# The adaLN modulation of a hybrid decoder layer as one-row matmuls in four column strips

## The chip, the cores and the metric

The kernel runs on one core of one Trainium2 chip. Its engines work beside each other from programs of their own: TensorE (PE, matmuls into the accumulators called PSUM; PEld is its weight load), VectorE (DVE), ScalarE (ACT), GpSimd (POOL, idle here) and SyncE (SP), which issues all DMAs here. The metric is the device time of one execution in microseconds (us); lower is better.

## The reference, cut to what matters

One decoder layer for 256 tokens of width 2048, all in float32:

```python
c_act = silu(c)                                   # (1, 2048)
mod = c_act @ w_ada + b_ada                       # w_ada: 2048 x 12288, 96 MB
sh1, sc1, g1, sh2, sc2, g2 = split(mod, 6)
h = layer_norm(x) * (1 + sc1) + sh1
mix = token_mix(h, ...)                           # w_in 2048 x 4160, attention (A), latent attention (B), w_o
x = layer_norm(alpha * x + g1 * mix)
h = layer_norm(x) * (1 + sc2) + sh2
ffn = peer(h, w_pq, sub_keys, u_table, v_table)   # 16384 experts of width 2048, top 16 of 8 heads
x = layer_norm(alpha * x + g2 * ffn)
```

The modulation is one row of 2048 numbers times a matrix: 12288 dot products, of which each number of the 96 MB of weights is read once.

## The kernel before, in words

The 2048 channels lie as 16 blocks of 128 on the partitions. The weights come in pieces of 1 MB. In most products a piece is split on the fly: ACT casts it to a short form `hi` (line 98), DVE forms the rest `lo` (line 100), and TensorE runs three matmuls of the short type for each product, hi by hi, lo by hi and hi by lo (`mm3`, lines 136 to 139). Some pieces go unsplit as float32 matmuls: 12 of the 32 pieces of `w_in` (`F32_PIECES`, line 330) and three of the latents' pieces (`LAT_F32`: uk0 and uq1 in line 154, uqr in line 147).

The modulation is done on DVE. `ada(pool, tag, bufs, j)` (line 203) loads the 1 MB of weights that make 128 of the 12288 outputs, with the outputs on the partitions, and multiplies it by silu(c), which `spread_cols` has spread over all partitions (`cb`), in two halves with a running sum (line 208). `ada_bias` (line 211) adds the halves and the bias into `modc`, one column for each block of 128 outputs. 32 such loads (shift 1 and scale 1) are needed before the rows of `w_in` that they modulate; 48 (gate 1, shift 2, scale 2) are drawn one by one at fixed places through attention and the output projection by `ada_pull`, from two buffers; 16 (gate 2) come in the second half of the kernel.

`w_in` is worked off in four groups `kg` of 512 of its 2048 rows. `group_start` modulates four blocks of the normalised input (ACT, line 301), splits them (lines 157 and 158) and multiplies them by the 64 columns of `w_kr` (line 306, result with the tokens on the partitions in two PSUM banks). `w_in_pieces` then multiplies eight pieces; after each, `ada_in` takes up one load of the next group's modulation. Attention follows with projections between its heads, then `w_o`, the norm, `w_pq`, the expert tables `u` (lines 132, 133) and `v`.

A scheduler orders the instructions of each engine when the program is built, and each engine then runs its list strictly in that order. A tile's buffer is handed on when its last reader is done: for a modulation weight that is DVE before the change.

Of the kernel before, what the change touches and what calls it, by code (L numbers as in the profile page):

```python
# [10 lines left out]
F32 = mybir.dt.float32  # L11
# [50 lines left out]
def tile_hybrid_peer_block(ctx: ExitStack, tc: tile.TileContext, a, out):  # L62
# [5 lines left out]
    psum = ctx.enter_context(tc.tile_pool(name="psum", bufs=2, space=PSUM))  # L68

    def bank(tag, name):  # L70
        return psum.tile([P, 512], F32, tag=tag, name=name, bufs=4 if tag == "mm" else 2)

    def banks8(name):
        return [bank(("mm", "mm", "mm", "mm", "tr", "tr", "sm", "sm")[i], f"{name}{i}") for i in range(8)]

    def bcast_row(dst, src_row):
        n = dst.shape[-1]
# [125 lines left out]
    def ada(pool, tag, bufs, j):  # L203

        w = pool.tile([P, D], F32, tag=tag, name=f"ada{j}", bufs=bufs).rearrange("p (z n) -> p z n", z=2)
        nc.sync.dma_start(w, a["w_ada"][j].rearrange("p (z n) -> p z n", z=2))
        for z in range(2):
            nc.vector.scalar_tensor_tensor(w[:, z, :], w[:, z, :], 1.0, cb[:, z * 1024:(z + 1) * 1024], op0=ALU.mult,  # L208
                                           op1=ALU.mult, accum_out=(modc, modh)[z][:, j:j + 1])

    def ada_bias(j0, n):
# [26 lines left out]

    with tc.tile_pool(name="front", bufs=1) as front:
        def ada_rest():  # L240
            for j in range(G1, SH2):
                ada(front, "ada", 2, j)
                yield
            ada_bias(G1, 16)
            for kg in range(4):
                for i in range(4):
                    for j0 in (SH2, SC2):
                        ada(front, "ada", 2, j0 + 4 * kg + i)
                        yield
                for j0 in (SH2, SC2):  # L250
                    ada_bias(j0 + 4 * kg, 4)

        rest = ada_rest()

# [17 lines left out]
        with tc.tile_pool(name="mix", bufs=1) as mix, ExitStack() as attn_pool:  # L272
# [9 lines left out]
            nc.scalar.activation(cols[:, V_C:V_C + KC], cols[:, V_C:V_C + KC], AF.Silu)  # L282
            spread_cols(cb, cols[:, V_C:V_C + KC], "c")
            for th in range(2):
                mv, r = ln_stats(mix, xn[th])
# [8 lines left out]
            def modulate(kg, h, kw, half):  # L294
                hs = slice(2 * half, 2 * half + 2)
                ks = slice(4 * kg + 2 * half, 4 * kg + 2 * half + 2)
                for j0 in (SH1, SC1):
                    ada_bias(j0 + 4 * kg + 2 * half, 2)
# [10 lines left out]
            kr_ps = [bank("sm", f"kr_ps{th}") for th in range(2)]  # L309

            def w_in_pieces(kg, ns, act):

# [33 lines left out]
            def ada_in(kg, m):  # L346
# [5 lines left out]
                    return ada(mix, f"xt{m % 2}", 1, j)  # L352
                return ada((early_a, early_b)[m % 2], "raw", 1, j)

            def group_start(kg):
# [15 lines left out]
            for m in range(4, 8):  # L371
                ada_in(0, m)
            for kg in range(3):
                h = group_start(kg)
                m = 0
                for ns in IN_ORDER[kg]:
                    w_in_pieces(kg, ns, h)
                    while m < ns[-1] + 1:
                        ada_in(kg + 1, m)
                        m += 1  # L380
            early_pools.close()
            hmod3 = group_start(3)

# [131 lines left out]
            def latents():  # L515
                w_in_pieces(3, (6, 7), hmod3)
                ada_pull(PULLS[0])
                krd = mix.tile([P, 2, 2, 64], F32, tag="kw", name="krd")
                for th in range(2):
                    nc.scalar.copy(krd[:, th, 0, :], kr_ps[th][:, :64])  # L520
# [9 lines left out]
                krT = attn.tile([P, T], F32, name="krT")  # L530
# [228 lines left out]
    with tc.tile_pool(name="back", bufs=1) as back:  # L759
# [24 lines left out]
        with tc.tile_pool(name="sel", bufs=1) as sel:  # L784
# [108 lines left out]
            def scatter(th, on_vector):  # L893

                for tb in range(8 * th, 8 * th + 8):
                    stg = sel.tile([P, NKEY, 16], F32, tag="stg", name=f"stg{tb}", bufs=2)
                    for b in range(4):
                        ps = bank(("sm", "tr")[b % 2], f"g_ps{tb}_{b}")
# [196 lines left out]
def _layout(i):  # L1095
    def tiles(w, n):
# [11 lines left out]
        "consts": _consts(),  # L1108
        "cols": cont(cols.T),
        "x": cont(i["x"].reshape(2, P, D)),  # L1110
        "w_ada": cont(i["w_ada"][0].reshape(D, 96, P).transpose(1, 2, 0)),
        "w_in": tiles(w_in[:, :4096], 512),
        "w_kr": cont(w_in[:, 4096:].reshape(4, 4, P, 64).transpose(0, 2, 1, 3)),
# [28 lines left out]
```

## Time and profile before

| | |
|---|---|
| three timed runs | 2072.48, 2075.01, 2075.48 us; median 2075.01 us |
| the profiled execution | 2072.09 us, its span 2070.3 us |
| TensorE busy, clock granted | 2002.6 us (97%), 0.983 |
| DVE, ACT busy | 1434.0 us (69%), 1027.9 us (50%) |
| HBM read | 473.40 MB |

Busy time of TensorE overstates its work, because matmuls are pipelined and their ends are modelled; what a matmul costs in a stream is the distance from start to start. A float32 matmul call stands in the trace as two records (each with its own weight load): the 96 calls of line 330 are 192 records. The granted clock is given as a share of 2.4 GHz; at 0.5 it is 1.2 GHz. "Who waited for whom" lists idle time of an engine with what ended it.

### The profile page before, as it was taken

How to read it: one execution, taken by the hardware profiler on the slowest of the kernel's cores; microseconds unless marked ns; L12 is line 12 of the kernel's file. 1: busy time of each engine (PE TensorE's matmuls, PEld its weight loads, DVE VectorE, ACT ScalarE, POOL GpSimd, SP SyncE). 2: the span in 40 equal slices, each digit the busy share in tenths (PEclk: the TensorE clock that was granted, in tenths of full speed). 3: DMA queues.
4: the chain of work that ended last, by engine and by line, in shares of the span. 5: the costliest groups of instructions: out<-in, count | busy, mean ns of one | idle time of the engine just before them, and what ended most of it. 6: DMA issues, size and time to landing. Idle time of an engine off the chain costs nothing.

```text
span 2070.3 us, 26806 instructions
## 1 busy us (share of the span) xinstructions
PE 2002.6 (97%) x10328; PEld 1672.8 (81%) x10329; DVE 1434.0 (69%) x2509; ACT 1027.9 (50%) x1478; POOL 0.2 (0%) x4
## 2 busy tenths in 40 slices
PE   6999998979999999999999999999999999999997
PEld 3567686769988888899888888888888888888886
DVE  7589978889799677677765454477766555445457
ACT  2323457445554877866444444454444454444441
POOL 0000000000000000000000000000000000000000
PEclk8999999989999999999999999999999999999999
DMA  9787887858445555666885555578876656555552
GB/s 364 314 328 311 328 323 262 345 234 318 184 157 190 194 212 193 224 204 214 291 280 190 198 188 198 188 266 306 300 286 244 224 205 235 192 202 184 203 203 102
DMA packets 100864, 496.13 MB, mean 240 GB/s; under 512 B 7792, under 2 KB 41728, under 8 KB 42880
## 3 DMA queue, kind: packets, MB, share of 16 engines
q1 hardware_dynamic: 100736, 494.41, 64.8%
q8 instruction: 81, 1.33, 0.2%
q14 instruction: 47, 0.39, 0.1%
HBM read 473.40 MB, written 20.98 MB: 239 GB/s over the span
## 4 chain that ended last, share of the span: by engine, by line
PE 93%; DVE 5%; ACT 1%; issue 0%; DMA 0%; SPq 0%; DVEq 0%; ACTq 0%
PE u_ps L132 23%; PE u_ps L133 12%; PE v_ps L138 11%; PE v_ps L137 11%; PE v_ps L139 11%; PE win_ps L330 3%; PE g_ps L914 3%; PE win_ps L138 2%; PE win_ps L139 2%; PE wpq_ps L138 2%; PE wpq_ps L139 2%; DVE ada L208 2%; PE wpq_ps L137 1%; PE win_ps L137 1%; PE wo_ps L139 1%; PE wo_ps L138 1%
## 5 line engine op out<-in xcount | busy, mean ns | idle before, releaser
L132 PE MATMUL u_ps<-act,hi_u 128*128 128x512 f32 x2048 | 727.8, 400 | 3.0 <-DVE W L779 3.0
L133 PE MATMUL u_ps<-act,lo_u 128*128 128x256 f32 x2048 | 574.0, 280 | 0.0
L100 DVE TENSOR_TENSOR lo_v<-raw_v,hi_v 128x1024 fp32r<-128x1024 f32 x244 | 298.2, 1224 | 264.4 <-ACT hi_v L98 264.3
L132 PEld LDWEIGHTS u_ps<-act,hi_u 128*128 128x128 f32 x2048 | 386.1, 189 | 95.2 <-DVE W L779 3.3
L100 DVE TENSOR_TENSOR lo_u<-raw_u,hi_u 128x1024 fp32r<-128x1024 f32 x256 | 312.1, 1222 | 179.8 <-ACT hi_u L98 178.8
L98 ACT CAST hi_v<-raw_v 128x1024 fp32r<-128x1024 f32 x244 | 257.2, 1054 | 327.8 <-PE v_ps L139 321.3
L133 PEld LDWEIGHTS u_ps<-act,lo_u 128*128 128x128 f32 x2048 | 387.6, 189 | 0.0
L137 PE MATMUL v_ps<-hi_v,whi 128*128 128x512 f32 x976 | 379.7, 389 | 0.0
L138 PE MATMUL v_ps<-lo_v,whi 128*128 128x512 f32 x976 | 379.7, 389 | 0.0
L139 PE MATMUL v_ps<-hi_v,wlo 128*128 128x512 f32 x976 | 379.7, 389 | 0.0
L98 ACT CAST hi_u<-raw_u 128x1024 fp32r<-128x1024 f32 x256 | 267.6, 1048 | 212.5 <-PE u_ps L132 193.4
L208 DVE SCALAR_TENSOR_TENSOR ada<-ada,cb 128x1024 f32<-128x1024 f32 x192 | 229.0, 1219 | 12.2 <-DMA ada<-in_w_ada_dram 12.0
L137 PEld LDWEIGHTS v_ps<-hi_v,whi 128*128 128x128 f32 x976 | 183.2, 188 | 38.3
L139 PEld LDWEIGHTS v_ps<-hi_v,wlo 128*128 128x128 f32 x976 | 183.2, 188 | 38.0
L138 PEld LDWEIGHTS v_ps<-lo_v,whi 128*128 128x128 f32 x976 | 183.2, 188 | 37.8
L330 PE MATMUL win_ps<-raw_win,hmod 128*128 128x512 f32 x192 | 87.2, 610 | 1.2 <-ACT hmod L301 1.2
L912 DVE TENSOR_SCALAR o<-iota,i2T,gT 128x128 f32<-128x128 f32 x256 | 72.9, 342 | 19.9 <-PE g_ps L914 19.8
L137 PE MATMUL wpq_ps<-act,hi_wpq 128*128 128x256 f32 x256 | 72.7, 286 | 1.9 <-ACT act L157 1.9
L138 PE MATMUL wpq_ps<-act,hi_wpq 128*128 128x256 f32 x256 | 73.1, 286 | 0.4 <-DVE act L158 0.4
L778 ACT COPY W<-u_ps 128x256 f32<-128x256 f32 x128 | 47.3, 369 | 52.3 <-PE u_ps L133 51.8
L139 PE MATMUL wpq_ps<-act,lo_wpq 128*128 128x256 f32 x256 | 72.8, 285 | 0.0
L330 PEld LDWEIGHTS win_ps<-raw_win,hmod 128*128 128x128 f32 x192 | 36.9, 196 | 43.8 <-issue 42.0
(319 smaller groups left out, 2316.1 us busy)
## 6 DMA issues: line engine op xcount, KB each, us to landing
raw_u<-in_u_dram SPq DMA_DIRECT2D x128, 1024.0 KB, 4.8
raw_v<-in_v_dram SPq DMA_DIRECT2D x122, 1024.0 KB, 4.8
ada<-in_w_ada_dram SPq DMA_DIRECT2D x96, 1024.0 KB, 5.9
raw_win<-in_w_in_dram SPq DMA_DIRECT2D x32, 1024.0 KB, 8.4
raw_wo<-in_w_o_dram SPq DMA_DIRECT2D x16, 1024.0 KB, 6.9
raw_wpq<-in_w_pq_dram SPq DMA_DIRECT2D x16, 1024.0 KB, 6.0
g_d<-stg SPq DMA_DIRECT2D x16, 1024.0 KB, 4.9
gl<-g_d SPq DMA_DIRECT2D x16, 1024.0 KB, 6.8
```

What stands on the lines that cost most here:

```text
L98: nc.scalar.copy(hi, raw[:, 2 * j:2 * j + 2, :])
L100: nc.vector.tensor_sub(lo, raw[:, 2 * j:2 * j + 2, :], hi.bitcast(F32))
L132: nc.tensor.matmul(pss[e], hi[:, i, es], act[:, k], start=first and j == 0 and i == 0, stop=False)
L133: nc.tensor.matmul(pss[e][:, 1], lo[:, i, es], act_hi[:, k, :], start=False, stop=last and j == 1 and i == 3)
L137: nc.tensor.matmul(o, sh, mh, start=start, stop=False)
L138: nc.tensor.matmul(o, sh, ml, start=False, stop=False)
L139: nc.tensor.matmul(o, sl, mh, start=False, stop=stop)
L208: nc.vector.scalar_tensor_tensor(w[:, z, :], w[:, z, :], 1.0, cb[:, z * 1024:(z + 1) * 1024], op0=ALU.mult, op1=ALU.mult, accum_out=(modc, ...
L330: nc.tensor.matmul(ps[th], act[:, i, ts], src[:, i, :], start=i == 0, stop=i == 3)
L778: nc.scalar.copy(ws[:, e], pss[e][:, 1])
L912: nc.vector.tensor_scalar(o2, iota, i2T[:, t:t + 1], gT[:, t:t + 1], op0=ALU.is_equal, op1=ALU.mult)
L914: nc.tensor.matmul(ps[:, q * P:(q + 1) * P], o1[:, q, :], o2, start=True, stop=True)
```

## The change

All of the modulation but gate 2 (80 of the 96 loads) becomes matmuls with one output row. silu(c) of one block of 128 channels is the stationary operand, one column wide, and 512 columns of a row block of `w_ada` stream by. Four row blocks write to output partitions 0, 32, 64 and 96 of one PSUM bank (the four column strips), and four 1 MB tiles, of four row blocks each, accumulate there. ACT copies the bank to SBUF, four matmuls by a matrix of ones and zeros (`strips`) add the four rows up and turn the result from a row into columns, and one DVE instruction adds the bias. That is a group: 512 outputs, 4 tiles, 16 matmuls, 1 copy, 4 small matmuls, 1 DVE instruction. There are 18 groups; the first 1024 outputs come from eight tiles in another cut (`first_ada`, 64 matmuls of 256 columns).

Further: 2 instead of 12 pieces of `w_in` and none of the latents stay float32; the product with `w_kr` is turned round (64 output rows by 256 tokens, two column halves in one bank), with a repair for its layout in `latents`; the PSUM bank thus freed holds the modulation. The weights are laid out anew for this on the host, with the same bytes.

```diff
-F32_PIECES = (4, 3, 2, 3)
+F32_PIECES = (2, 0, 0, 0)
-LAT_F32 = ('uk0', 'uq1', 'uqr')
+LAT_F32 = ()
...
-        return psum.tile([P, 512], F32, tag=tag, name=name, bufs=4 if tag == "mm" else 2)
+        return psum.tile([P, 512], F32, tag=tag, name=name, bufs={"mm": 4, "tr": 2, "sm": 1, "ad": 1}[tag])
...
+    def ada_group(ps, ws, tiles, strips, j0):
+        for q in range(4):
+            p, tag, bufs = tiles[q]
+            w = p.tile([P, 4, 512], F32, tag=tag, name=f"ada{j0}_{q}", bufs=bufs)
+            nc.sync.dma_start(w, ws[q])
+            for g in range(4):
+                nc.tensor.matmul(ps[32 * g:32 * g + 1, :], c1[:, 4 * q + g:4 * q + g + 1], w[:, g, :], start=q == 0,
+                                 stop=q == 3)
+            if q < 3:
+                yield
+        rows = stream.tile([P, 2, 512], F32, tag="lo", name=f"ada_rows{j0}", bufs=4)[:, 0, :]
+        nc.scalar.copy(rows, ps)
+        yield
+        for i in range(4):
+            nc.tensor.matmul(ps[:, 2 * i:2 * i + 2], rows[:, i * P:(i + 1) * P], strips[:, 2:4], start=True, stop=True)
+        one = 1.0 if (SC1 <= j0 < G1 or SC2 <= j0 < G2) else 0.0
+        nc.vector.scalar_tensor_tensor(modc[:, j0:j0 + 4], ps[:, 0:8:2], one, cols[:, j0:j0 + 4], op0=ALU.add,
+                                       op1=ALU.add)
...
         def ada_rest():
-            for j in range(G1, SH2):
-                ada(front, "ada", 2, j)
-                yield
-            ada_bias(G1, 16)
...
+            order = [G1 + 4 * g for g in range(4)] + [j + 4 * g for g in range(4) for j in (SH2, SC2)]
+            for j0 in order:
+                yield from ada_group(ada_ps, a["w_ada_r"][j0 // 4], [(front, "ada", 2)] * 4, strips, j0)
...
                 for i in range(2 * half, 2 * half + 2):
-                    for th in range(2):
-                        nc.tensor.matmul(kr_ps[th][:, :64], h[:, i, th * P:(th + 1) * P], kw[:, i, :],
-                                         start=(kg == 0 and i == 0), stop=(kg == 3 and i == 3))
+                    g = 64 * (i % 2)
+                    nc.tensor.matmul(kr_ps[g:g + 64, :T], kw[:, i, :], h[:, i, :], start=(kg == 0 and i < 2),
+                                     stop=(kg == 3 and i >= 2))
...
+            def first_ada(half):
...
+                    for which in range(2):
+                        ada_rows(ps, ws[which], which, part)
...
-            for m in range(4):
-                ada_in(0, m)
+            first_ada(0)
...
             for kg in range(3):
                 h = group_start(kg)
                 m = 0
+                if ON_PE:
+                    slots = [(front, "ada", 2)] * 2 + [(mix, f"xt{m}", 1) for m in range(2)]
+                    work = [ada_group(ada_ps, a["w_ada_r"][j0 // 4 + kg + 1], slots, strips, j0 + 4 * kg + 4)
+                            for j0 in (SH1, SC1)]
+                    work = itertools.chain(*work)
                 for ns in IN_ORDER[kg]:
                     w_in_pieces(kg, ns, h)
                     while m < ns[-1] + 1:
-                        ada_in(kg + 1, m)
+                        if ON_PE:
+                            next(work, None)
```

Where the work moves on TensorE shows in its list, in which a number after an L is a line of its own kernel (lines 138 to 140 after are `mm3`, 137 to 139 before). First the passage from group 0 of `w_in` to group 1, before: `win_ps` are the products with `w_in`, `kr_ps` those with `w_kr`.

```order
L139 MATMUL win_ps_7_1_498<-hi_win_7_1_505,act 128x512
L306 MATMUL kr_ps_232<-kw_540,hmod_539 128x64 [waits DMAHW5_49]
L306 MATMUL kr_ps_233<-kw_540,hmod_539 128x64
L306 MATMUL kr_ps_232<-kw_540,hmod_539 128x64 [waits Activation_49]
L330 MATMUL win_ps_0_0_566<-raw_win_0_572,hmod_539 128x512 [waits DMAHW6_49]
```

After, in the same place; `ada_ps` is the bank of the modulation, `ada_rows` its copy in SBUF:

```order
L140 MATMUL win_ps_7_1_626<-hi_win_7_1_633,act 128x512
L233 MATMUL ada_ps<-ada_3_663,cols 1x512 [waits DMAHW4_49]
L233 MATMUL ada_ps<-ada_3_663,cols 1x512 x3
L241 MATMUL ada_ps<-strips,ada_rows_669 128x2 [waits Activation_49]
L241 MATMUL ada_ps<-strips,ada_rows_669 128x2 x3
L344 MATMUL kr_ps<-hmod_676,kw_677 64x256 [waits DMAHW5_49,Activation_49]
L138 MATMUL win_ps_0_0_691<-hi_win_0_0_699,act 128x512 [waits Activation_49]
L139 MATMUL win_ps_0_0_691<-lo_win_0_0_701,act 128x512 [waits DVE_49]
```

The last tile of the modulation that group 1 needs, and its strips, stand directly ahead of the group's own products. Second, the start of the latent attention heads, before: `s_b` are scores, `uv_ps` a projection ahead of them.

```order
L139 MATMUL uv_ps_1853<-hi_uv_1_1860,act 128x512
L561 MATMUL s_b_1894<-qk_1180 128x128 [waits Activation_49]
L562 MATMUL s_b_1894<-krT,qk_1180 128x128
L563 MATMUL s_b_1894<-qk_1180 128x256
L564 MATMUL s_b_1894<-krT,qk_1180 128x256
L561 MATMUL s_b_1934<-qk_1180 128x128 [waits Activation_49]
```

After, with the tiles of one group of the modulation between the heads:

```order
L140 MATMUL uv_ps_2322<-hi_uv_1_2329,act 128x512
L233 MATMUL ada_ps<-ada_1_2359,cols 1x512 [waits DMAHW3_49]
L639 MATMUL s_b_2365<-qk_1461 128x128 [waits Activation_49]
L640 MATMUL s_b_2365<-krT,qk_1461 128x128
L641 MATMUL s_b_2365<-qk_1461 128x256
L642 MATMUL s_b_2365<-krT,qk_1461 128x256
L233 MATMUL ada_ps<-ada_2_2391,cols 1x512 [waits DMAHW6_49]
L639 MATMUL s_b_2416<-qk_1461 128x128 [waits Activation_49]
```

Each tile's four matmuls stand alone between matmuls of full width, and wait for their own load. Over the whole list TensorE changes between calls of different shape of the array (128 rows by 128, 64 or 32 columns, or 64 rows) 34 times before and 198 times after.

## Rows read from the trace of the kernel before

**Rows 1.** The page's head: span, busy time by engine, clock in 40 slices.

```profile
span 2070.3 us, 26806 instructions
...
PE 2002.6 (97%) x10328; PEld 1672.8 (81%) x10329; DVE 1434.0 (69%) x2509; ACT 1027.9 (50%) x1478; POOL 0.2 (0%) x4
...
PEclk8999999989999999999999999999999999999999
```

**Rows 2.** The page's chain that ended last, share by engine.

```profile
PE 93%; DVE 5%; ACT 1%; issue 0%; DMA 0%; SPq 0%; DVEq 0%; ACTq 0%
```

**Rows 3.** Windows: stretch, length, busy us (count) by engine, clock, DMA share, GB/s.

```profile
45.00:250.00 205.00, 197.99 (x732) 132.55 (x731) 166.25 (x284) 71.72 (x104) 0.00 (x0) 0.98 0.80 322
250.00:325.00 75.00, 74.14 (x408) 58.04 (x407) 60.71 (x167) 41.49 (x99) 0.00 (x0) 1.00 0.81 314
325.00:475.00 150.00, 125.37 (x577) 99.79 (x577) 130.11 (x278) 83.53 (x138) 0.00 (x0) 0.91 0.72 282
475.00:600.00 125.00, 121.82 (x934) 118.55 (x935) 109.41 (x349) 59.74 (x73) 0.00 (x0) 0.96 0.60 227
600.00:2071.00 1471.00, 1458.05 (x7583) 1246.42 (x7581) 933.27 (x1351) 758.11 (x1044) 0.00 (x0) 1.00 0.61 218
```

**Rows 4.** Timeline of TensorE, float32 `w_in` pieces: start, length, count.

```profile
91.96 20.82 PE L330 MATMUL win_ps<-raw_win,hmod 128*128 128x512 f32 x48
```

**Rows 5.** Line 330 by itself: count, duration min/median/max in ns.

```profile
L330 PEld LDWEIGHTS win_ps<-raw_win,hmod x192: 186/190/337, 28.2 to 235.6; 128*128 128x128 f32 x192
L330 PE MATMUL win_ps<-raw_win,hmod x192: 591/592/1167, 28.2 to 236.0; 128*128 128x512 f32 x192
```

**Rows 6.** Windows, `win_ps` alone, split pieces only.

```profile
116.00:136.00 20.00, 20.00 (x90) 16.56 (x89) 4.80 (x7) 0.00 (x0) 1.00 0.97 388
```

**Rows 7.** Timeline of TensorE, a split projection of 256 columns.

```profile
263.13 0.28 PE L137 MATMUL uq_ps<-act,hi_uq 128*128 128x256 f32 x1
...
265.53 0.28 PE L139 MATMUL uq_ps<-act,lo_uq 128*128 128x256 f32 x1
```

**Rows 8.** Timeline of TensorE at the passage to group 1: the product with w_kr.

```profile
90.23 1.89 PE L306 MATMUL kr_ps<-kw,hmod 128*128 128x64 f32 x16
```

**Rows 9.** Timeline of TensorE, scores of latent heads; 64*128 is half the array's rows.

```profile
284.27 0.49 PE L562 MATMUL s_b<-krT,qk 64*128 64x128 f32 x2
284.69 0.70 PE L563 MATMUL s_b<-qk 128*128 128x256 f32 x2
285.32 0.70 PE L564 MATMUL s_b<-krT,qk 64*128 64x256 f32 x2
285.94 0.49 PE L561 MATMUL s_b<-qk 128*128 128x128 f32 x2
```

**Rows 10.** Instruction groups of DVE up to 700 us: the modulation.

```profile
L208 DVE SCALAR_TENSOR_TENSOR ada<-ada,cb 128x1024 f32<-128x1024 f32 x160 | 190.9, 1219 | 10.0 <-DMA ada<-in_w_ada_dram 9.8
```

**Rows 11.** Who waited for whom, TensorE, 45 to 600 us: total, times, longest.

```profile
PE h_ps L712 <- ACT xc L709: 10.7, 2, 6.9
PE win_ps L138 <- DVE lo_win L100: 5.6, 4, 2.9
PE pt_a L434 <- DVE mx_a L429: 4.9, 4, 3.6
```

**Rows 12.** Timeline, all engines, second half of group 0's modulation.

```profile
39.76 0.16 DVE L215 SCALAR_TENSOR_TENSOR modc<-modc,cols 128x2 f32<-128x2 f32 x1
39.95 1.09 ACT L301 ACTIVATE hmod<-xnT,modc 128x256 f32<-128x256 f32 x2 [10.70 <-DVE modc L215]
...
41.08 0.62 ACT L157 CAST act<-hmod 128x512 fp32r<-128x512 f32 x1
...
41.73 0.69 DVE L158 TENSOR_TENSOR act<-hmod,act 128x512 fp32r<-128x512 f32 x1 [1.81 <-ACT act L157]
...
50.46 0.59 ACT L340 COPY proj<-win_ps 128x512 f32<-128x512 f32 x1 [8.76 <-PE win_ps L330]
```

**Rows 13.** DMA issues of the page: count, KB each, median us to landing.

```profile
ada<-in_w_ada_dram SPq DMA_DIRECT2D x96, 1024.0 KB, 5.9
```

More of the change, by code (lines that the diff above doesn't have):

```diff
@@ L70, in bank @@
     def bank(tag, name):
-        return psum.tile([P, 512], F32, tag=tag, name=name, bufs=4 if tag == "mm" else 2)
+        return psum.tile([P, 512], F32, tag=tag, name=name, bufs={"mm": 4, "tr": 2, "sm": 1, "ad": 1}[tag])
     def banks8(name):
-        return [bank(("mm", "mm", "mm", "mm", "tr", "tr", "sm", "sm")[i], f"{name}{i}") for i in range(8)]
+        return [bank(("mm", "mm", "mm", "mm", "tr", "tr", "sm", "ad")[i], f"{name}{i}") for i in range(8)]
     def bcast_row(dst, src_row):
@@ L209, in ada, with silu_strips, ada_rows @@
                                            op1=ALU.mult, accum_out=(modc, modh)[z][:, j:j + 1])
+    c1 = cols[:, V_C:V_C + KC]
+    def silu_strips(pool):
+        ps = bank("ad", "ada_ps")
+        nc.vector.memset(ps, 0.0)
+        strips = pool.tile([P, 4], F32, name="strips")
+        nc.vector.memset(strips, 0.0)
+        for g in range(4):
+            nc.vector.memset(strips[32 * g:32 * g + 1, g // 2:g // 2 + 1], 1.0)
+            nc.vector.memset(strips[32 * g:32 * g + 1, 2:4], 1.0)
+        return ps, strips
+    def ada_group(ps, ws, tiles, strips, j0):
[3 more added lines that the diff above has]
+            nc.sync.dma_start(w, ws[q])
+            for g in range(4):
+                nc.tensor.matmul(ps[32 * g:32 * g + 1, :], c1[:, 4 * q + g:4 * q + g + 1], w[:, g, :], start=q == 0,
[10 more added lines that the diff above has]
+                                       op1=ALU.add)
+    def ada_rows(ps, w, which, half):
+        for i in range(8):
+            g = 32 * (2 * which + i % 2)
+            k = 8 * half + i
+            nc.tensor.matmul(ps[g:g + 1, :256], c1[:, k:k + 1], w[:, i, :], start=half == 0 and i < 2,
+                             stop=half == 1 and i >= 6)
     def ada_bias(j0, n):
@@ L297, in modulate @@
                 for j0 in (SH1, SC1):
-                    ada_bias(j0 + 4 * kg + 2 * half, 2)
+                    if kg > 0 and not ON_PE:
+                        ada_bias(j0 + 4 * kg + 2 * half, 2)
                 for i in range(2 * half, 2 * half + 2):
@@ L304, in modulate @@
                 for i in range(2 * half, 2 * half + 2):
[L305 to L309 removed]
+                    g = 64 * (i % 2)
+                    nc.tensor.matmul(kr_ps[g:g + 64, :T], kw[:, i, :], h[:, i, :], start=(kg == 0 and i < 2),
+                                     stop=(kg == 3 and i >= 2))
+            kr_ps = bank("sm", "kr_ps")
             def w_in_pieces(kg, ns, act):
@@ L353, in ada_in @@
                 return ada((early_a, early_b)[m % 2], "raw", 1, j)
+            def first_ada(half):
+                ps = ada_ps
+                for part in range(2):
+                    ws = []
+                    for which in range(2):
+                        m = 4 * half + 2 * part + which
+                        where = (0, 2, 1, 0)[m // 2]
+                        pool, tag, bufs = ((front, "ada", 2), (mix, f"xt{m % 2}", 1),
+                                           ((early_a, early_b)[m % 2], "raw", 1))[where]
+                        w = pool.tile([P, 8, 256], F32, tag=tag, name=f"ada0_{m}", bufs=bufs)
+                        nc.sync.dma_start(w, a["w_ada0"][half, which, part])
+                        ws.append(w)
+                    for which in range(2):
+                        ada_rows(ps, ws[which], which, part)
+                rows = stream.tile([P, 2, 512], F32, tag="lo", name=f"first_rows{half}", bufs=4)[:, 0, :]
+                nc.scalar.copy(rows[:, :256], ps[:, :256])
+                for i in range(2):
+                    nc.tensor.matmul(ps[:, 256 + 2 * i:258 + 2 * i], rows[:, i * P:(i + 1) * P], strips[:, 0:2], start=True,
+                                     stop=True)
+                for which, (j0, one) in enumerate(((SH1, 0.0), (SC1, 1.0))):
+                    j = j0 + 2 * half
+                    nc.vector.scalar_tensor_tensor(modc[:, j:j + 2], ps[:, 256 + which:260:2], one, cols[:, j:j + 2],
+                                                   op0=ALU.add, op1=ALU.add)
             def group_start(kg):
@@ L366, in tile_hybrid_peer_block @@
             early_b = early_pools.enter_context(tc.tile_pool(name="early_b", bufs=1))
-            for m in range(4):
-                ada_in(0, m)
+            first_ada(0)
             for n in range(2):
                 first[0, n] = load_piece(a["w_in"][0, n], f"win0_{n}")
-            for m in range(4, 8):
-                ada_in(0, m)
+            first_ada(1)
             for kg in range(3):
@@ L378, in tile_hybrid_peer_block @@
                     while m < ns[-1] + 1:
-                        ada_in(kg + 1, m)
+                        if ON_PE:
+                            next(work, None)
+                        else:
+                            ada_in(kg + 1, m)
                         m += 1
+                if ON_PE:
+                    for _ in work:
+                        pass
             early_pools.close()
@@ L518, in latents @@
                 krd = mix.tile([P, 2, 2, 64], F32, tag="kw", name="krd")
+                krs = attn.tile([P, T], F32, name="krT")
+                nc.scalar.copy(krs, kr_ps[:, :T])
+                both = attn.tile([P, 64], F32, name="both")
+                nc.vector.tensor_add(both, ident[:, 0:64], ident[:, 64:128])
                 for th in range(2):
-                    nc.scalar.copy(krd[:, th, 0, :], kr_ps[th][:, :64])
+                    nc.tensor.matmul(kr_ps[:, 256 + th * 64:320 + th * 64], krs[:, th * P:(th + 1) * P], both, start=True,
+                                     stop=True)
+                    nc.scalar.copy(krd[:, th, 0, :], kr_ps[:, 256 + th * 64:320 + th * 64])
                 nc.sync.dma_start(cst, a["consts"][:, C_COSA:])
```

16 lines of the change are left out of this document (7 added, 9 removed).

## The prediction, made before the kernel was run

> **What bounds the kernel now.** I read the page's head first, then its chain, then windows by stage, then rows of single lines. TensorE is busy 97% of the span and its clock is granted nearly throughout [rows 1]; the chain that ended last is TensorE for 93% [rows 2]. A busy share can hide idle time, so the test is the distance from start to start: 48 float32 records take 20.82 us, less the last one's own 0.59 that is 0.430 us each [rows 4, 5], and 90 records of the split pieces start in 20.00 us, 0.222 us each [rows 6]. Those streams are dense; no faster engine beside them would shorten them. The windows say where TensorE has idle time after its start: 7.0 us from 45 to 250, 0.9 to 325, 24.6 to 475, 3.2 to 600 [rows 3], 35.7 us in all. DVE works 190.9 us on the modulation [rows 10], but of TensorE's waits those that end with DVE come to 5.6 and 4.9 us; the longest total, 10.7, ends with ACT [rows 11]. DVE is full, and yet hardly in the way.
>
> So 190.9 us are taken from an engine with little on the path, and work is put on the engine that is the path. Everything hangs on how much TensorE time the column strips take.
>
> **The change part by part.** The sum is made on the profiled execution's 2072.09 us, 2.9 under the median of 2075.01.
>
> *Float32 pieces become split ones.* A piece was 8 calls, 16 records: 16 x 0.430 = 6.88 us. Split it is 24 x 0.222 = 5.33. Ten pieces of w_in and uqr save 1.55 each, 17.1 us. uk0 and uq1 have 256 columns: 32 records at half of 0.430 are 6.88; split they are 48 at 0.120 (20 steps in 2.40 us [rows 7]), 5.76; two save 2.2. Together -19.3. ACT and DVE get the casting of 13 pieces more; DVE has the room, since it loses 190.9.
>
> *The product with w_kr.* 64 records at 1.89/16 = 0.118 [rows 8] were 7.6 us. Now 16 calls of 256 columns, 32 records at 0.215, are 6.9 one after the other and 3.4 if the two halves run beside each other as I assume below for the strips. -4 (bounds -0.7 to -6).
>
> *The strips.* The first 1024 outputs wait for their loads before and after: 0. The other 18 groups have 72 tiles, each four calls of 512 columns. A float32 call is two records (192 for 96 calls [rows 5]), both on the same strip. No row of before shows a narrow call, so I bound a tile. One after the other its 8 records take 8 x 0.430 = 3.44 us. With four strips fully side by side only the two passes of one strip are left: 0.86. Between them lies what TensorE's order makes likely: records start in the order of the program, and the second pass of strip 0 stands ahead of the first of strip 32 and needs strip 0 free. Then each call adds one pass, not a quarter: first pass, then four steps, 5 x 0.430 = 2.15 us. I take that: 72 x 2.15 = +155 us; the ends are +62 and +248.
>
> The Trainium skill (TensorE: Matmul & The Clock Gate, section on packing small matmuls) says that matmuls start and end strictly in program order, and gives 2.38x for three column strips measured. The order would give my middle value; the speedup, taken as 3x for four strips, gives about 1.15 us a tile, 83 us, and an end some 72 us earlier. No row here shows strips, so neither is tested yet.
>
> *Change of shape.* Where full calls alternate with calls on half of the rows, two records of 256 columns take 0.63 and 0.62 us from start to start instead of 0.43 [rows 9]: 0.2 us for each change of shape. The list has 198 such changes instead of 34. 164 x 0.2 = +33 us (bounds 0, if columns differ from rows in this, and 33).
>
> *Adding up.* Four calls for each group with two columns by a full weight load, 144 records; the nearest row is w_kr's narrow call at 0.118 [rows 8]: +17 (bounds 8 and 31, at 0.215).
>
> *New waits.* The last tile of a group of w_in now stands directly ahead of that group's products. From the bias to the split input took 2.5 us (39.92 to 42.42 [rows 12]), and ACT's copy of the bank, 0.59 for that shape [rows 12], comes ahead of it; the products with w_kr fill about a half of a microsecond. Before, those products followed without a gap [rows 8]. I take 3 us at each of three passages: +9 (bounds 3 and 15). In the list a tile also waits for its load, which takes 5.9 us [rows 13], with two buffers that come free only when TensorE has read them. Queued behind it is all of TensorE. Between uv and the heads three tiles stand close together, and likewise near w_pq. The single bank makes the next group wait for DVE's bias. I take +10 (bounds 0 and 25; the end is 12 groups at about 2 us).
>
> *Given back.* Some tiles fall into the 35.7 idle microseconds [rows 3], and waits for DVE shrink. -25 (bounds 0 and -36). What is late next in those places is ACT, which ends the longest wait [rows 11].
>
> Sum: -19.3 - 4 + 155 + 17 + 33 + 9 + 10 - 25 = +175.7. 2072.1 + 175.7 = 2248.
>
> **Rivals.**
>
> *Four strips at once* (27%). The passes of different strips overlap fully, 0.86 a tile. For it: the list gives consecutive calls to different strips, and the array's columns are not shared. Against: the second pass of each call stands in the way, in a list run in order. It saves 155 - 62 = 93: 2155.
>
> *No overlap* (18%). Each call of one output row takes what a full call takes, 3.44 a tile. For it: 0.430 a record is the time for 512 columns to stream by, however many output rows there are. Against: nothing but that different strips are different columns. It adds 93: 2341. The Trainium skill, in the section named above, lets a weight load overlap a running matmul only where the row group differs; all four strips use all rows, so by that rule nothing would overlap. In this trace the rule does not hold as it stands: line 330's weight loads of 0.190 us, all on full rows, vanish in a distance of 0.430 [rows 4, 5]. I give the case no more for it.
>
> *Not slower* (9%, 2061). One mechanism, at the tile: both passes of all four strips run in the time of one pass, 0.43. Then the strips cost 31, and with the change of shape free, no new wait, and all idle time filled the sum is -19 - 4 + 31 + 17 - 36 = -11. It decides below about 0.58 us a tile, where those terms reach zero. For it: the waits for DVE exist. Against: a second pass on the same columns at the same time is what no row shows.
>
> The likeliest (46%) is the middle one; its own range, from the smaller bounds, is 2205 to 2285.
>
> **How the numbers follow.** The range for 8 times in 10 reaches from below the case of four strips at once to the case of no overlap: 2115 to 2345, with the upper half of the no-overlap case and all of the not slower one left out. Faster and no change come from the last rival alone: 0.06 and 0.03; slower 0.91. (0.2% is about 4 us, roughly what a measurement of this kernel can tell from no change.)
>
> **What would show each step.** In the timeline the four calls of a tile, eight records: 2.15 us from the first to the next matmul of full width confirms the middle case, 0.86 and 3.44 the others; the second pass of a strip starting with the first of the next shows the order at work. A split call next to a strip 0.2 us late confirms the change of shape. DVE's busy time must fall by about 191 less 13 x 2 x 1.22 = 32. The windows up to the expert phase must hold the whole difference: after it the same matmuls run at the same distance. The forecast is wrong if a tile takes under a microsecond, or if TensorE's idle time before 600 us grows by tens of microseconds through loads, which would be a wait that I priced at 10.

## The result and the profile after

| | before | after |
|---|---|---|
| median (lowest to highest), us | 2073.74 (2071.52 to 2075.48), 4 runs | 2160.11 (2158.52 to 2164.52), 4 runs |
| ratio after to before | | 1.042, 95% interval 1.0401 to 1.044 |
| span of the profiled execution, us | 2070.3 | 2157.4 |
| TensorE, DVE, ACT busy, us | 2002.6, 1434.0, 1027.9 | 2102.1, 1284.5, 1066.7 |

The kernel became 86 us slower. The direction was forecast, the size was not: the forecast was 2248 us, +176, twice what was measured. The page's head after, against [rows 1], and the chain's shares, against [rows 2]:

```profile
span 2157.4 us, 28515 instructions
...
PE 2102.1 (97%) x11276; PEld 1710.5 (79%) x11277; DVE 1284.5 (60%) x2198; ACT 1066.7 (49%) x1525; POOL 0.2 (0%) x4
...
PEclk9999999998899999999999999999999999999999
...
PE 90%; DVE 4%; DMA 4%; ACT 2%; issue 1%; DVEq 0%; SPq 0%; ACTq 0%
```

DVE lost 149.5 us of work, TensorE gained 99.5, and TensorE was the chain before and still is. What is new in the chain is DMA, 4% where [rows 2] have 0%. The dent in the granted clock is two slices long, the 10th and 11th, 485 to 593 us, where [rows 1] show one, the 9th, besides the first.

To see where the 86 us lie, mark the same instructions in both traces (start of a tile's first or last matmul, us):

| | before | after | later by |
|---|---|---|---|
| first product with w_kr | 37.3 | 40.9 | 3.7 |
| last of w_in | 247.5 | 271.4 | 23.9 |
| last scores of a latent head (`s_b`) | 324.8 | 371.9 | 47.1 |
| last of w_o's first three column blocks | 450.7 | 507.2 | 56.5 |
| last of w_pq | 573.5 | 659.5 | 86.0 |
| end | 2070.3 | 2157.4 | 87.1 |

All of it lies ahead of the expert phase, as forecast. The windows of the same stages after, in the columns of [rows 3], up to the expert phase:

```profile
45.00:274.00 229.00, 224.07 (x1106) 151.65 (x1104) 115.44 (x158) 99.90 (x136) 0.00 (x0) 1.00 0.77 298
274.00:372.00 98.00, 96.83 (x617) 67.25 (x616) 34.98 (x123) 50.74 (x116) 0.00 (x0) 1.00 0.63 237
372.00:532.00 160.00, 144.37 (x733) 99.99 (x732) 95.63 (x202) 82.06 (x131) 0.00 (x0) 0.96 0.70 269
532.00:660.00 128.00, 119.94 (x900) 106.73 (x900) 64.56 (x189) 50.32 (x62) 0.00 (x0) 0.92 0.49 178
```

Length less PE's busy time is TensorE's idle time: 4.9, 1.2, 15.6 and 8.1 us, 29.8 in all, against 35.7 in [rows 3]. So idle time did not grow in sum; the loss is busy time. In the last of these windows two things are worse than in its counterpart of [rows 3]: 8.1 us idle, where 3.2 had been, and a clock of 0.92, where it had been 0.96.

**What a tile costs.** The timeline of TensorE around one tile (start, length, count; L138 to L140 are split products):

```profile
73.47 0.39 PE L140 MATMUL win_ps<-hi_win,act 128*128 128x512 f32 x1
73.78 1.04 PE L233 MATMUL ada_ps<-ada,cols 128*1 128x512 f32 x8
74.75 0.50 PE L138 MATMUL win_ps<-hi_win,act 128*128 128x512 f32 x1
75.09 0.39 PE L139 MATMUL win_ps<-lo_win,act 128*128 128x512 f32 x1
```

In a dense stream the split products start 0.227 us apart. (The 0.222 of [rows 6] is a little low: of its 90 records two had begun before the window; 88 start in it.) From the split product ahead of the tile to the second one behind it are 1.62 us, which without the tile would be 2 x 0.227. The tile costs 1.17 us, with both changes of shape, where I had 2.15 and 0.4. Three short windows on the tile's line alone show its inside (the first count is that of the TensorE records at work in the window, the second that of their weight loads):

```profile
73.70:73.85 0.15, 0.07 (x4) 0.07 (x8) 1.00 1.57 655
73.85:74.15 0.30, 0.30 (x4) 0.04 (x8) 1.00 1.05 437
74.15:74.30 0.15, 0.15 (x8) 0.00 (x0) 1.00 0.39 164
```

In the first 70 ns four records have started, and no other starts for 0.3 us; then the other four start while the first four end. By the single records the starts are 0, 7, 13 and 20 ns, then 428, 435, 442 and 448. In the program each call's two passes stand one behind the other, each behind its own weight load. All eight weight loads begin in the first window, but only four matmuls do: the engine has reached the end of the tile's list while the second passes still wait. So the first passes of all four strips run side by side, and then the second passes (that it is not both passes of two strips follows from e3, where passes on one strip start 0.43 us apart). That is 0.86 us of streaming. The other 0.31 us are the two changes of shape: the tile's first record starts 0.09 us late, the first product behind the tile 0.09, the second another 0.11.

Not every tile stands in one stretch. Between the first call of eleven of the 72 and their other three calls the scheduler has put other matmuls, as here between two heads:

```profile
363.16 1.02 PE L233 MATMUL ada_ps<-ada,cols 128*1 128x512 f32 x2
364.11 0.49 PE L510 MATMUL o_b<-vb,pt_b 128*128 128x128 f32 x2
365.09 1.03 PE L233 MATMUL ada_ps<-ada,cols 128*1 128x512 f32 x6
```

The lone call takes as long as the other three together, since its two passes follow each other with three strips empty. Eleven times 0.86 us are 9.5 us of streaming that the count of tiles does not show; as other tiles stand next to each other, there are 73 stretches in all.

**The passage to a group of w_in.** TensorE at the start of group 1, against the dense passage of [rows 8]; the brackets are idle time and what ended it:

```profile
93.70 1.04 PE L233 MATMUL ada_ps<-ada,cols 128*1 128x512 f32 x8
95.45 1.05 PE L241 MATMUL ada_ps<-strips,ada_rows 128*128 128x2 f32 x8 [0.70 <-ACT ada_rows L238]
97.46 1.63 PE L344 MATMUL kr_ps<-hmod,kw 128*64 128x256 f32 x6 [0.96 <-ACT hmod L339]
```

The new wait is there, 0.70 + 0.96 = 1.66 us, about half of the 3 that I had. Over the whole of w_in TensorE's waits for `ada_rows` and `hmod` sum to 4.6 us. The adding-up takes 1.05 us a group, 18 x 1.05 = 18.9 us (forecast 17).

**Around w_pq.** SyncE's own queue, and TensorE's wait for the tiles' loads from 500 to 660 us:

```profile
536.77 25.86 SPq L231 DMA_DIRECT2D ada<-in_w_ada_r_dram  x5
562.72 7.33 SPq L83 DMA_DIRECT2D raw_wpq<-in_w_pq_dram  x3
```

```profile
PE ada_ps L233 <- DMA ada<-in_w_ada_r_dram: 6.3, 2, 3.3
```

A tile's load may start only when one of its two buffers has been read by TensorE. SyncE needs 26 us to get out five such loads, and the pieces of w_pq, issued by the same queue, come behind them. The timeline of TensorE in this stretch, and a window with its clock:

```profile
555.06 1.04 PE L233 MATMUL ada_ps<-ada,cols 128*1 128x512 f32 x8 [3.03 <-DMA ada<-in_w_ada_r_dram]
556.81 1.71 PE L241 MATMUL ada_ps<-strips,ada_rows 128*128 128x2 f32 x8 [0.71 <-ACT ada_rows L238]
560.36 1.88 PE L233 MATMUL ada_ps<-ada,cols 128*1 128x512 f32 x8
```

```profile
558.00:563.00 5.00, 5.00 (x23) 3.07 (x23) 3.56 (x4) 0.00 (x0) 0.00 (x0) 0.50 0.43 177
```

From 558 to 563 us, behind the two waits, the clock is granted at 0.50, its lower level of 1.2 GHz, and the tile at 560.36 takes 1.88 us instead of 1.04.

### The profile page after: what moved, and what is told of

Read it like the earlier page. It is cut to its first block, busy times and chain, and to the rows that moved or that the text cites. A ratio compares the mean times of both kernels' runs of the same rounds, so it can differ in the third digit from the quotient of the medians.

```text
span 2157.4 us, 28515 instructions
## 1 busy us (share of the span) xinstructions
PE 2102.1 (97%) x11276; PEld 1710.5 (79%) x11277; DVE 1284.5 (60%) x2198; ACT 1066.7 (49%) x1525; POOL 0.2 (0%) x4
## 3 DMA queue, kind: packets, MB, share of 16 engines
q8 instruction: 88, 1.44, 0.3%
## 4 chain that ended last, share of the span: by engine, by line
PE 90%; DVE 4%; DMA 4%; ACT 2%; issue 1%; DVEq 0%; SPq 0%; ACTq 0%
PE u_ps L133 21%; PE u_ps L134 11%; PE v_ps L139 10%; PE v_ps L140 10%; PE v_ps L138 10%; PE ada_ps L233 3%; PE g_ps L992 3%; PE win_ps L138 3%; DMA gl<-g_d 3%; PE win_ps L139 3%; PE win_ps L140 3%; PE wpq_ps L140 1%; PE wpq_ps L138 1%; PE wpq_ps L139 1%; PE wo_ps L140 1%; PE wo_ps L138 1%
## 5 line engine op out<-in xcount | busy, mean ns | idle before, releaser
L138 PE MATMUL v_ps<-hi_v,whi 128*128 128x512 f32 x976 | 379.9, 389 | 0.0
L140 PE MATMUL v_ps<-hi_v,wlo 128*128 128x512 f32 x976 | 379.7, 389 | 0.0
L138 PEld LDWEIGHTS v_ps<-hi_v,whi 128*128 128x128 f32 x976 | 183.2, 188 | 38.5 <-DVE W L857 0.3
L140 PEld LDWEIGHTS v_ps<-hi_v,wlo 128*128 128x128 f32 x976 | 183.2, 188 | 37.9
L99 ACT CAST hi_win<-raw_win 128x1024 fp32r<-128x1024 f32 x60 | 62.5, 1051 | 86.1 <-PE win_ps L140 84.4
L101 DVE TENSOR_TENSOR lo_win<-raw_win,hi_win 128x1024 fp32r<-128x1024 f32 x60 | 72.0, 1221 | 47.5 <-ACT hi_win L99 47.5
L233 PE MATMUL ada_ps<-ada,cols 128*1 128x512 f32 x576 | 88.5, 611 | 7.3 <-DMA ada<-in_w_ada_r_dram 6.3
L138 PE MATMUL win_ps<-hi_win,act 128*128 128x512 f32 x240 | 95.2, 404 | 0.0
L139 PE MATMUL win_ps<-lo_win,act 128*128 128x512 f32 x240 | 94.5, 394 | 0.0
L140 PE MATMUL win_ps<-hi_win,act 128*128 128x512 f32 x240 | 93.9, 391 | 0.0
L138 PE MATMUL wpq_ps<-act,hi_wpq 128*128 128x256 f32 x256 | 74.8, 295 | 0.0
```

Of the source, the lines that this page charges most:

```text
L99: nc.scalar.copy(hi, raw[:, 2 * j:2 * j + 2, :])
L101: nc.vector.tensor_sub(lo, raw[:, 2 * j:2 * j + 2, :], hi.bitcast(F32))
L138: nc.tensor.matmul(o, sh, mh, start=start, stop=False)
L139: nc.tensor.matmul(o, sh, ml, start=False, stop=False)
L140: nc.tensor.matmul(o, sl, mh, start=False, stop=stop)
L233: nc.tensor.matmul(ps[32 * g:32 * g + 1, :], c1[:, 4 * q + g:4 * q + g + 1], w[:, g, :], start=q == 0, stop=q == 3)
```

## The experiments

Ratios are to the kernel before, run on the same chip; after has 1.042. Differences in us are from the median of after, those of e2 and e10 from that of before beside them. The kernel before had medians of 2070.21 to 2073.74 us beside the four sets of runs, so such a difference is sure to about 4 us.

| kernel | median, us | ratio (95% interval) |
|---|---|---|
| e1_float32_back | 2184.04 | 1.0552 (1.0528 to 1.0575) |
| e2_split_alone | 2087.63 | 1.008 (1.0058 to 1.0102) |
| e3_one_strip | 2309.24 | 1.1149 (1.1124 to 1.1175) |
| e4_two_strips | 2214.25 | 1.0695 (1.0671 to 1.0719) |
| e5_narrow | 2121.13 | 1.0242 (1.0223 to 1.0261) |
| e6_rest_no_loads | 2142.01 | 1.034 (1.0322 to 1.0357) |
| e7_rest_early | 2168.12 | 1.0459 (1.0441 to 1.0478) |
| e8_rest_vector | 2099.09 | 1.0124 (1.0104 to 1.0143) |
| e9_groups_vector | 2150.76 | 1.0383 (1.0365 to 1.0401) |
| e10_kr_alone | 2072.31 | 1.0001 (0.9991 to 1.0012) |
| e11_quarter_strips | 2149.96 | 1.0378 (1.036 to 1.0396) |
| e12_three_buffers | 2148.47 | 1.0372 (1.0354 to 1.039) |

### How many strips: e3 and e4

```diff
# e3: one strip                                    # (strips' ones in row 0 alone)
-                nc.tensor.matmul(ps[32 * g:32 * g + 1, :], ...
+                nc.tensor.matmul(ps[0:1, :], ...
# e4: two strips, two calls after another on each  # (ones in rows 0 and 64)
+                s = 64 * (g // 2)
+                nc.tensor.matmul(ps[s:s + 1, :], ...
```

> After, with all four matmuls of a tile on output partition 0, so that they queue for one column strip, in the 72 tiles behind the first 1024 outputs; the same sums come out. Theory (the strips run side by side, which holds a tile at 0.86 us of streaming): eight records one after the other are 3.44 us, 72 x 2.58 = +186, 2346 us. Rival (a one-row call is short whatever its strip, and waits around the tiles make the 86 us): within 10 us of 2160.

> After, with two strips instead of four: a tile's first two matmuls on partition 0, the next two on partition 64. Two calls a strip are four records, 1.72 us if the strips run side by side. Theory (TensorE looks past records that wait for their strip, so that strip 64 starts at once): +72 x 0.86 = +62, 2222 us, and in the timeline the third call starts with the first. Rival (records start in the order of the program, and strip 64 begins only when the last pass of strip 0 begins): 1.29 + 1.72 = 3.01 us a tile, +155, 2315 us.

The same places of TensorE's timeline, one strip first, then two:

```profile
72.90 0.39 PE L140 MATMUL win_ps<-hi_win,act 128*128 128x512 f32 x1
73.22 3.59 PE L233 MATMUL ada_ps<-ada,cols 128*1 128x512 f32 x8
76.75 0.73 PE L138 MATMUL win_ps<-hi_win,act 128*128 128x512 f32 x2
```

```profile
67.58 0.39 PE L140 MATMUL win_ps<-hi_win,act 128*128 128x512 f32 x1
67.90 1.89 PE L235 MATMUL ada_ps<-ada,cols 128*1 128x512 f32 x8
69.72 0.73 PE L138 MATMUL win_ps<-hi_win,act 128*128 128x512 f32 x2
```

The two products behind a tile are again 0.34 us apart (the 0.73 of the two less the last one's own 0.39). By the same subtraction a tile costs 3.73 us on one strip, 2.04 on two and 1.17 on four: 3.43, 1.72 and 0.86 of streaming, halved each time, and 0.3 for the changes of shape, the same in all three. In e4 the second record to start does so 13 ns after the first. It must be strip 64's, since in e3 passes on one strip start 0.43 us apart; yet three records of strip 0 stand ahead of it in the program and still wait. (In after strip 32's first record, two places down the list, started after 7 ns; strip 64's here, four places down, after 13.) TensorE thus starts records past others whose strip is busy; the rival of e4, which is the order that my forecast rested on, is excluded. Of the whole, +149 came of e3's +186 and +54 of e4's +62. Each group of w_in was longer by the full price in e3 (77 to 79 us from start to start, after 57 to 59; 8 tiles x 2.56 = 20.5); w_pq, with eight tiles too, was not (138 us from the norm's last transposes, after 132). There TensorE's idle time fell from 10.2 to 5.2 us, and the clock rose from 0.91 to 0.99; the line of after stands below with e6, this is e3's:

```profile
672.00:811.00 139.00, 133.78 (x913) 106.77 (x914) 64.46 (x189) 54.14 (x70) 0.00 (x0) 0.99 0.49 173
```

### The streaming: e5

```diff
-                nc.tensor.matmul(ps[32 * g:32 * g + 1, :], c1[...], w[:, g, :], ...
+                nc.tensor.matmul(ps[32 * g:32 * g + 1, :32], c1[...], w[:, g, :32], ...
```

> After, with only the first 32 of the 512 columns of each row block multiplied in the 72 tiles; the other 480 columns of the modulation behind the first 1024 outputs are left out, while loads, waits, changes of shape, copies and strips stay. Theory (a tile's price is its streaming, 0.86 us, plus about 0.2 us for two changes of shape): nearly all of the streaming goes, 72 x 0.75 = -54, 2106 us. Rival (what is dear about a tile is the waiting around it: loads, changes of shape, the bank): under 25 us less, 2135 to 2160 us.

-39 us, between the two expectations. The other 480 columns of each row block are left out. The tile itself shrank as the theory said, to 0.49 + 0.34 - 2 x 0.227 = 0.38 us, so 72 x 0.79 = 57 us of work went:

```profile
72.32 0.39 PE L140 MATMUL win_ps<-hi_win,act 128*128 128x512 f32 x1
72.64 0.24 PE L233 MATMUL ada_ps<-ada,cols 128*1 128x32 f32 x8
72.81 0.73 PE L138 MATMUL win_ps<-hi_win,act 128*128 128x512 f32 x2
```

18 us of it did not reach the end. TensorE's idle time from the first product with w_kr to the last of w_pq rose beside it, from 30.2 to 48.9 us, and in it the waits for these tiles' loads, to 13.6 us (6.3 after):

```profile
PE ada_ps L233 <- DMA ada<-in_w_ada_r_dram: 13.6, 4, 5.4
```

### The loads: e6, e7 and e12

```diff
# e6: the 48 tiles behind the w_in groups use two loads
+            if held is not None and len(held) == 2:
+                w = held[q % 2]
# e7
-PULL_WO = (2, 3, 0, 1, 1, 1, 1, 1, 0, 0, 1, 2)
+PULL_WO = (3, 4, 1, 2, 2, 2, 2, 2, 1, 1, 2, 3)
# e12: the third place is that of cb, the spread silu(c), now made only in the second half
+            ring = [(front, "ada", 2), (front, "ada", 2), (base, "third", 1)]
```

> After, with the 48 tiles for gate 1, shift 2 and scale 2 taken from two tiles that are loaded once; the loads of the other 46 are left out, and those tiles multiply the wrong weights. Theory (around w_pq TensorE waits for loads that its own two buffers hold up, and w_pq's pieces queue behind them on SyncE): -10 to -20, 2140 to 2150 us, nearly all of it between the end of w_o and the end of w_pq. Rival (those loads are hidden, and w_pq is longer through the tiles and strips themselves): 2154 to 2162 us.

> After, with the last tiles of the modulation drawn earlier, eleven more of them during w_o, so that hardly any are left for w_pq. Theory (at w_pq the tiles meet the loads of its pieces, a bank that w_pq itself wants, and half clock): w_pq becomes some 20 us shorter, w_o some 10 us longer for the tiles themselves, about 2148 us. Rival (each tile costs the same wherever it stands): within 4 us of 2160.

> After, with a third buffer for the 48 tiles of gate 1, shift 2 and scale 2: the place of the spread silu(c), which is now spread only in the second half, where gate 2 still needs it. Theory (two buffers let TensorE wait for loads around w_pq, which cost 18 us by the run without loads): most of that comes back, 2144 to 2150 us, and TensorE's waits for these loads go from 6 us towards nothing. Rival (SyncE's queue, in which those loads hold up w_pq's pieces whenever their buffer is not free, is the limit, whatever the number of buffers): 2154 to 2162 us.

e6 leaves out 46 loads: -18, as the theory had it. The windows from the norm's last transposes to the end of w_pq, after and e6, the columns as above:

```profile
527.00:660.00 133.00, 122.80 (x913) 108.87 (x912) 64.56 (x189) 54.38 (x70) 0.00 (x0) 0.91 0.49 178
```

```profile
532.00:643.00 111.00, 110.97 (x903) 101.68 (x903) 63.65 (x186) 52.72 (x66) 0.00 (x0) 0.99 0.42 147
```

Without the loads TensorE is never idle there (10.2 us after) and its clock is 0.99. Of the 22 us some 10 were idle time and some 11 the clock (133 x 0.09 less 111 x 0.01); DMA is only half busy in both, so it is not bandwidth but who waits for whom.

e7 met neither expectation: w_pq came back to its length of before, and yet the whole was 8 us slower.

```profile
566.00:670.00 104.00, 101.65 (x828) 100.25 (x828) 63.66 (x186) 52.71 (x66) 0.00 (x0) 0.98 0.46 166
```

But from the start of w_o to the norm's last transposes it took 172.0 us (134.9 after). That stretch in after and in e7:

```profile
392.00:527.00 135.00, 123.89 (x620) 87.59 (x622) 84.02 (x151) 62.37 (x90) 0.00 (x0) 0.97 0.73 281
394.00:566.00 172.00, 142.40 (x705) 93.99 (x707) 85.23 (x155) 63.92 (x94) 0.00 (x0) 0.90 0.67 258
```

Eight tiles more (22 for 14) and three groups' adding-up explain some 12 of these 37 us. TensorE's idle time explains 18 (29.6 for 11.1), with the longest wait for the normalised rows at 10.6 us (6.3). The clock, 0.90 for 0.97, accounts for what is left. So the tiles bring waits and the lower clock to the place where they are put; why the wait for the normalised rows grew stays open.

e12: -12 by the medians, -7 by the profiled spans. w_pq is 21 us shorter, and TensorE's waits for the loads are down to 0.2 us from 45 to 700 us. SyncE's own waits before these loads, from 500 to 620 us, are those of after or more (after first, then e12):

```profile
PE ada_ps L232 <- DMA ada<-in_w_ada_r_dram: 0.2, 1, 0.2
```

```profile
SPq L231 <- PE ada_ps L233: 31.4, 9, 13.1
SPq L230 <- PE ada_ps L232: 35.8, 7, 12.2
```

```profile
401.00:543.00 142.00, 127.08 (x620) 92.56 (x619) 85.17 (x153) 63.30 (x91) 0.00 (x0) 0.92 0.68 265
543.00:654.00 111.00, 110.97 (x901) 101.35 (x901) 62.99 (x185) 53.04 (x66) 0.00 (x0) 0.98 0.53 194
```

So the buffers, not SyncE's queue as such, made the waits at w_pq: the queue stands as long, and TensorE no longer waits. The stages ahead were together 15 us longer, some 4 us each in w_in, the heads, w_o and the norm. From w_o to the norm (the first of the two lines, against after's above) TensorE is idle for 14.9 us where it was 11.1, and the clock is 0.92 where it was 0.97; in w_in and the heads the clock is 0.98 where it was 1.00. Why the clock fell more often in e12 stays open.

### The two halves of the change: e1, e2, e8, e9

```diff
# e1 (in after); e2 is the reverse, in before
-F32_PIECES = (2, 0, 0, 0)
+F32_PIECES = (4, 3, 2, 3)
-LAT_F32 = ()
+LAT_F32 = ('uk0', 'uq1', 'uqr')
# e8: ada_rest as before the change
# e9
-ON_PE = True
+ON_PE = False
```

> The changed kernel with the twelve float32 pieces of w_in and the three of the latents put back; all else as after. Theory (TensorE is the bound before the expert phase, and split passes are shorter there): the 19.3 us of the forecast come back, 2160 + 19 = 2179 us, and DVE is about 32 us less busy. Rival (the casting of 13 pieces more, on ACT and DVE, sits on the path, so the exchange gave little): 2155 to 2166 us.

> The kernel before with the other half of the change alone: two float32 pieces of w_in left, none of the latents; the modulation stays on DVE. Theory (TensorE is the bound, DVE has room for 32 us more in a span that is 69% busy): -19, 2055 us. Rival (in the w_in groups DVE was busy 166 of 205 us, and 27 us more there fill it): TensorE waits for lo parts, 2065 to 2085 us.

> After, with the 48 loads for gate 1, shift 2 and scale 2 back on DVE as before the change, in their places; the first 32 stay on TensorE, and nearly all pieces stay split. Theory (tiles, strips and their waits make the 62 us that the stages from attention to w_pq have lost): those stages return to the kernel before but for a few us that DVE lacks, 2160 - 58 = 2102 us. Rival (DVE, with the casting of the split pieces on top, becomes the bound there): 2115 to 2145 us.

> After, with the modulation of groups 1 to 3 of w_in back on DVE, in the places it had before; the first tiles and the 48 for gate 1, shift 2 and scale 2 stay on TensorE, and nearly all pieces stay split. Theory (24 tiles at 1.06 us, six passages of strips and a wait at each group): those go, about 40 us, but DVE then lacks about 12 us in w_in as where split pieces stood alone: 2160 - 28 = 2132 us. Rival (with DVE busy in w_in those stages are bound by DVE and as long as now): 2150 to 2165 us.

e1: the float32 pieces cost after 20 us by the profiled spans (2177.4 against 2157.4) and 24 by the medians; the forecast's 19.3 holds. e2: the same exchange on DVE's old load is no gain but a loss of 17. Its w_in stage, with TensorE idle 21 of 217 us (7.0 of 205 in [rows 3]) and DVE busy 87%, and the wait that ended most of it:

```profile
45.00:262.00 217.00, 196.00 (x818) 151.16 (x816) 187.81 (x310) 92.28 (x125) 0.00 (x0) 0.96 0.77 309
```

```profile
PE win_ps L138 <- DVE lo_win L100: 13.2, 13, 3.8
```

So the two halves belong together: split pieces pay only once DVE is relieved, and relieving it in this way costs more than they pay. e8: with the 48 later loads back on DVE -61, as the theory had it; the stages from the end of w_in to that of w_pq return nearly to their old length (329.5 us; 326.1 before, 388.0 after). e9: with the 24 loads of groups 1 to 3 on DVE only -9, as the rival had it; with split pieces DVE is busy for 170 of the 217 us from 45 to 262, and TensorE waits 11.7 us for `lo` there instead of working on tiles.

### The small parts: e10 and e11

```diff
# e10: in before, the turned product with w_kr and its repair, as in the change
# e11
-        for i in range(4):
+        for i in range(1):
             nc.tensor.matmul(ps[:, 2 * i:2 * i + 2], rows[:, i * P:(i + 1) * P], strips[:, 2:4], ...
```

> The kernel before with the turned product with w_kr alone (and its repair in the latents). Theory (32 records of 256 columns for 64 narrow ones): -4, about 2068 us. Rival (its changes of shape and the repair, which lies between TensorE and ACT, cost what it saves): 2071 to 2078 us.

> After, with one of the four small matmuls that add up each of the 18 groups; the other three are left out, so that three quarters of the modulation behind the first 1024 outputs are wrong. Theory (each small call costs TensorE its two records, about 0.12 us each): 54 x 0.25 = -13, 2147 us. Rival (TensorE waits for ACT's copy at that place, and the calls themselves fit into waits for the group's input): within 4 us of 2160.

e10: no difference, so my -4 was 0. The product itself did get shorter, 1.02 us to the product behind it, after 1.73 before [rows 4, 8], where one after the other its eight records would take 8 x 0.215 = 1.72. So its two halves run side by side:

```profile
90.29 1.08 PE L306 MATMUL kr_ps<-hmod,kw 128*64 128x256 f32 x8
91.31 1.98 PE L330 MATMUL win_ps<-raw_win,hmod 128*128 128x512 f32 x4
```

What the repair and the rest of the way take back is not shown singly. e11 leaves out three of the four small matmuls of each group: -10 of the 13 expected, so all four would cost about 13 us at the end of the program, and 19 on TensorE.

## Why the prediction was wrong

**The step that failed** is the tile: "records start in the order of the program, and the second pass of strip 0 stands ahead of the first of strip 32 and needs strip 0 free ... 5 x 0.430 = 2.15 us". e4 shows that a record whose strip is busy does not hold back one of another strip. The tile streams for 0.86 us, the lower end of my bounds and my rival "four strips at once". The text ahead of the prediction says that each engine runs its list strictly in that order; for TensorE's records on different strips that is wrong. I called the rival the less likely because of that order; the Trainium skill (TensorE: Matmul & The Clock Gate, Part 3: Packing small matmuls, under The mechanism) states it for matmuls outright, and here the trace does not agree: a second pass of strip 0 starts at 428 ns, and a first pass of strip 32, later in the program, at 7 ns.

**The change of shape** went with it: 0.09 us into a tile and 0.2 out of it, 0.31 for the two where I took 0.4 from [rows 9], in which calls switch between all and half of the rows. With 72 x 0.86 = 62 us of streaming, 9.5 for the eleven divided tiles and 73 x 0.31 = 23 for the shapes, the tiles are 94 us where I had 155 + 33 = 188. I had 94 us too much there, more than the whole miss of 88; the rest of my sum was 6 us too low.

**Float32 to split**: -20 where I had -19, with the condition that e2 adds. (At 0.227 us a record three split passes save 1.44 us a piece, not 1.55, which would have made it -18.) **w_kr**: 0 for -4; [rows 8] have the next product 1.73 us behind, 0.108 a record and not 0.118, and the repair was priced at nothing. **Adding-up**: 19 for 17. **The start** I had at 0; it is 3.7.

**Waits.** The passages cost 4.6 us where I had 9. The loads I had at 10, with bounds 0 and 25; around w_pq they cost 18 (e6), by idle time and by the lower clock together. That half of a load's price can be a slower clock afterwards was not in my list. Yet in sum the waits came out near the forecast. From the first product with w_kr to the last of w_pq, before and after:

```profile
37.26:573.56 536.30, 502.04 (x2545) 393.06 (x2547) 444.81 (x961) 246.84 (x400) 0.00 (x0) 0.96 0.76 296
40.94:659.47 618.53, 588.30 (x3362) 426.72 (x3362) 310.99 (x672) 285.66 (x446) 0.00 (x0) 0.97 0.67 256
```

Idle time fell by 4 us (34.3 to 30.2), and what the clock took by 3 (536 x 0.04 less 618 x 0.03): -7 in all, where my new waits less what is given back were 9 + 10 - 25 = -6. With the loads at 18 and the passages at 4.6, some 30 us must have come back elsewhere; this is an estimate, and part of the agreement is luck.

So the account reads -20 + 0 + 94 + 19 - 7 + 4 = +90, of 86 measured. It is an estimate: its terms come from different runs, part of the lower clock falls into idle time, and e3, e5, e7 and e12 show that the terms do not simply add, since work taken from TensorE came back in part as waits.

**Right** were the bound (TensorE, 93% of the chain before and 90% after), the direction, DVE's relief (149.5 us; 191 - 32 = 159 forecast), that its waits had not been in the way, and that the whole difference lies before the expert phase. My rival of four strips at once said 2155, 5 us below the measured time. That it came so close is in part luck: its price for the shapes was 10 us too high, and it lacked the 9.5 of the divided tiles. None of these kernels beats the one before; e10 equals it, and the nearest with modulation on TensorE, e8, is 1.2% slower.

## What to carry to other kernels

Relieving an engine that ends few of the bound engine's waits returns only what its room lets another exchange earn, 20 us here, while the work moved costs its full time on the bound engine: about 94 us of tiles and 19 of adding-up, even with four strips at once. Calls that share the array must also stand together: a tile that the scheduler divides streams twice. When an unmeasured operation has bounds of 0.86 and 3.44 us, the way the program is written does not settle it; one run of the operation with its resource shared and one with it split (e3, e4) does. Where the busiest engine frees the buffers of a load, expect it to wait for its own loads, and the clock to fall on top; a third buffer took these waits away (e12), although the queue stood as long.

## What the runs showed of the hardware

- Column strips run fully side by side for float32: 3.43, 1.72 and 0.86 us of streaming for eight records of 512 columns on one, two and four strips. TensorE starts records of a free strip past waiting ones of another, 13 ns after the first past three of them (e4).
- The change from full calls to one-column calls costs 0.09 us and the change back 0.2, over the two products behind; that between all and half of the rows, 0.2 [rows 9].
- Behind two waits of 3.03 and 0.71 us TensorE's clock was granted at 0.50 from 558 to 563 us, and a tile took 1.88 us instead of 1.04; over the w_pq stage the mean was 0.91, and 0.99 without the loads (e6).
- A float32 piece is slower than its three split passes by 1.44 us (16 x 0.430 against 24 x 0.227), and yet the better choice where DVE makes the `lo` parts and is busy 87% of the stage (e2).
